# A one-core Strassen weight gradient: another visit order, one pair more, another queue for the last store

## The chip, the cores and the metric

The kernel runs on one core of a Trainium2 chip. TensorE (PE) does the matmuls, VectorE (DVE) and ScalarE (ACT) do the additions and copies, GpSimd (POOL) issues the converting loads, SyncE (SP) issues stores, and 16 DMA engines carry the data. The metric is the device time of one execution in microseconds; lower is better. The kernel before takes 166.42 us, the median of three runs from 166.34 to 166.46. The profile is one execution, whose span from first to last instruction is 164.9 us.

## What is computed

```python
def setup_inputs():
    batch, m, k, n = 16, 512, 1024, 768
    return {
        "input": np.random.randn(batch, m, k).astype(np.float32),
        "grad_output": np.random.randn(batch, m, n).astype(np.float32),
    }

def reference(input, grad_output):
    grad_weight = np.einsum('bmk,bmn->kn', input, grad_output)
    return grad_weight.astype(np.float32)
```

With X of 8192 x 1024 and G of 8192 x 768 this is one matrix product, X transposed times G, of 1024 x 768, contracted over 8192 rows.

## The kernel before, in words

**Output and blocks.** The output is cut into four quadrants of 512 x 384: A (top left), B (top right), C (bottom left), D (bottom right). Each has four pieces q of 128 rows. A piece of 128 x 384 in f32 fits one bank of PSUM; the eight banks make two slots of four, so two quadrants (or two of the Strassen products below) are open at a time. Sums that are not open rest in SBUF: `acc` for A to D, `macc` for the five products m, n, o, p, q.

**Items.** The contraction is cut into 32 units of 256 rows. The string `LOADS` says for each unit how it is used. A unit marked `s` gives two single items of 128 rows; each costs one matmul for each of the 16 pieces of the output, so 32 matmuls a unit. A unit marked `P` is a Strassen pair: its two halves of 128 rows and the two halves of X's and G's columns are the 2 x 2 blocks of one Strassen step, with seven products instead of eight. Each product has four pieces, so 28 matmuls a unit. Two of the products are added straight to A and D; the other five are gathered in m, n, o, p, q. For a pair, DVE first makes six operand sums: `sum_g1` to `sum_g3` of G's blocks and `sum_x1` to `sum_x3` of X's (lines 124 to 153). Products need some of them: m needs g2 and x2, n and q need x1, o and p need g3, A and D need x3 and g1.

**Loads.** GpSimd issues all loads but the first ones, and the DMA turns f32 into bf16. Units below `MERGED` are loaded in two halves of 128 rows (lines 110 and 112), later ones whole (lines 105 and 106). 14 units fit the ring of buffers. The first two tiles of X and the first of G come as f32 through SyncE's and ScalarE's queues and are rounded by DVE and ScalarE (`round_by`, line 202).

**The order.** All engines run in an order written out by hand in `ORDER`. A step such as `3D29!3,0,0,0` is one visit: take 3 operand sums from the list `filler` first, then multiply into D all of its items up to the 29th, then close (the `!`), that is, empty the four banks into SBUF; the four numbers say how many sums DVE takes in ahead of each piece's emptying. A number after a colon (`A28:2`) gives the last pieces of the visit to ScalarE: if the sum was there before, ScalarE copies it from SBUF into the bank ahead of the matmuls (the opening, line 267), and copies the bank back afterwards (line 291). The other pieces are added by DVE from the bank to SBUF (line 295), or copied by it the first time (line 293). A visit without `!` leaves the quadrant open for the next one.

**The end.** After the last pair the five products are shared out to the quadrants: `SHARES` lists 24 additions of `macc` to `acc`, on DVE. Each quadrant's last emptying is followed by its store, issued by SyncE (line 299). In the very last piece the columns are cut into 256 and 128, with one addition and one store each (lines 327, 335 and 336). Ten matmuls of 512 columns and two of 128 run at the start on a constant, to warm up TensorE's clock (line 88).

Of the kernel before, what the change touches and what calls it, by code (L numbers as in the profile page):

```python
# [1 line left out]

# [5 lines left out]

P = 128

LOADS = "ssssssssPPPPPPPPPPPPPPPPPPPPPsss"

ORDER = (
# [10 lines left out]
).split()  # L26


SHARES = (
    "t10 t11 t12 t13 l20 t20 t21 t22 t23 l21 l22 l23 l10 l11 l12 l13 l30 l31 l32 l33 t30 t31 t32 "  # L30
    "t33 "
).split()

WARMUP = [512] * 10 + [128] * 2
PAIRS_HELD = 14
SUMS_HELD = 9

MERGED = 7


@with_exitstack
def kernel(
# [6 lines left out]
    nc = tc.nc  # L49
# [4 lines left out]
    _, _, N = grad_output.shape  # L54
    S = B * M // P
    KH = K // 2
    NH = N // 2
    Q = KH // P
# [3 lines left out]
    OUT = out.rearrange("(ks p) n -> p ks n", p=P)  # L62
# [7 lines left out]
    acc = accp.tile([P, 2 * Q, N], f32, name="acc")  # L70

    macc = accp.tile([P, 5, Q, NH], f32, name="macc")
    SLOT = {"n": 0, "p": 1, "m": 2, "o": 3, "q": 4}
# [23 lines left out]
    items = []  # L97
# [56 lines left out]

    def settled(row, q):
        for p, (_, banks) in opened.items():
            assert p not in ("CD" if row else "AB") or not banks[q][1]

    def share(row, slots, q):
        settled(row, q)  # L160
        dst = acc[:, row + q, :].rearrange("p (h n) -> p h n", h=2)
        nc.vector.tensor_add(out=dst, in0=dst, in1=macc[:, slots, q, :])  # L162

    def top1(q):
        share(0, slice(2, 4), q)

    def top2(q):
        share(0, slice(1, 5, 3), q)

    def top3(q):  # L170
        settled(0, q)
        c = acc[:, q, 0:NH]
        nc.vector.tensor_sub(out=c, in0=c, in1=macc[:, 4, q, :])  # L173

    def low1(q):
        share(Q, slice(0, 3, 2), q)

    def low2(q):
        share(Q, slice(1, 4, 2), q)

    def low3(q):
        settled(Q, q)
        c = acc[:, Q + q, NH:N]
        nc.vector.tensor_sub(out=c, in0=c, in1=macc[:, 0, q, :])

    filler = []
    for i, item in enumerate(items):
        if item[0] == "P":
            filler += [(f, i) for f in (sum_g1, sum_g2, sum_g3, sum_x1, sum_x2, sum_x3)]
    share_by = {"t1": top1, "t2": top2, "t3": top3, "l1": low1, "l2": low2, "l3": low3}  # L190
    filler += [(share_by[c[:2]], int(c[2:])) for c in SHARES]
    filler.reverse()

    def fill(n):
# [20 lines left out]
    streams = {  # L215
        p: [i for i, item in enumerate(items) if item[0] in KINDS.get(p, "P")] for p in "ABCDmnopq"
    }

    LAST_PAIR = max([i for i, item in enumerate(items) if item[0] == "P"], default=0)

    def operands(p, i, q):
        kind, x, g = items[i]
# [16 lines left out]
    def sum_of(p, q):  # L239
        if p in SLOT:  # L240
            return macc[:, SLOT[p], q, :]
        row = q if p in "AB" else Q + q
        return acc[:, row, 0:NH] if p in "AC" else acc[:, row, NH:N]
# [3 lines left out]
    slots = [0, 1]  # L247
    used = set()

    def visit(p, upto, byact, close, ahead, last):  # L250
        items_now = streams[p][done[p] : upto]
        done[p] = upto
        opening = p not in opened
        if opening:

            tail = p in "ABCD" and streams[p][upto - len(items_now)] > LAST_PAIR - 2
            slot = slots.pop(0)
            banks = []
            for q in range(Q):
                name = f"bank{slot * Q + q}"  # L260
                bank = psum.tile([P, 512], f32, name=name)[:, 0:NH]
                act = q >= Q - byact
                carried = act and not fresh[p]
                assert not (carried and tail)
                if carried:
                    assert name in used
                    nc.scalar.copy(out=bank, in_=sum_of(p, q))  # L267
                used.add(name)
                banks.append((bank, carried, act))
            opened[p] = (slot, banks)  # L270
        slot, banks = opened[p]
        final = upto == len(streams[p])

        def mm(q, j):
            stat, mov = operands(p, items_now[j], q)
            bank, carried, _ = banks[q]
            nc.tensor.matmul(  # L277
                bank,
                stat,
                mov,  # L280
                start=opening and j == 0 and not carried,
                stop=close and j == len(items_now) - 1,
                skip_group_check=carried,
            )

        def shut(q):
            fill(ahead[q])
            bank, _, act = banks[q]
            dst = sum_of(p, q)
            if act:  # L290
                nc.scalar.copy(out=dst, in_=bank)  # L291
            elif fresh[p]:
                nc.vector.tensor_copy(out=dst, in_=bank)  # L293
            else:
                nc.vector.tensor_add(out=dst, in0=bank, in1=dst)  # L295
            if final and p in "ABCD":
                row = q if p in "AB" else Q + q
                c0 = 0 if p in "AC" else NH
                nc.sync.dma_start(out=OUT[:, row, c0 : c0 + NH], in_=dst)

        if len(items_now) == 1:
            for q in range(Q):
                mm(q, 0)
            if close:
                for q in range(Q):
                    shut(q)
        else:
            for q in range(Q):
                if last and q == Q - 1 and opening:
                    break  # L310
                for j in range(len(items_now)):
                    mm(q, j)
                if close:
                    shut(q)
            else:
                q = None
            if q is not None:

                fill(ahead[q])
                dst = sum_of(p, q)  # L320
                row = q if p in "AB" else Q + q
                b0 = 0 if p in "AC" else NH
                for c0, c1, name in ((0, 256, None), (256, NH, f"bank{slots[0] * Q}")):
                    bank = banks[q][0] if name is None else psum.tile([P, 512], f32, name=name)
                    for j in range(len(items_now)):
                        stat, mov = operands(p, items_now[j], q)
                        nc.tensor.matmul(
                            bank[:, 0 : c1 - c0],
                            stat,
                            mov[:, c0:c1],  # L330
                            start=j == 0,
                            stop=j == len(items_now) - 1,
                        )
                    d = dst[:, c0:c1]
                    nc.vector.tensor_add(out=d, in0=bank[:, 0 : c1 - c0], in1=d)  # L335
                    nc.sync.dma_start(out=OUT[:, row, b0 + c0 : b0 + c1], in_=d)
        if close:
            fresh[p] = False
            del opened[p]
            slots.append(slot)  # L340

    for n, step in enumerate(ORDER):
        step, _, ahead = step.partition("!")
        step, _, byact = step.partition(":")
        at = next(c for c in step if c.isalpha())
        before, upto = step.split(at)
        if n == 1:
            round_by("DVE", g0, gf, NH, N)
        if n == 2:
            round_by("DVE", x1, xf[1], 4 * P, 6 * P)  # L350
            round_by("ACT", x1, xf[1], 6 * P, 8 * P)
            round_by("DVE", x1, xf[1], 0, 2 * P)
            round_by("ACT", x1, xf[1], 2 * P, 4 * P)
        fill(int(before or 0))
        ahead = [int(a) for a in ahead.split(",")] if ahead else None
        visit(at, int(upto), int(byact or 0), ahead is not None, ahead, n == len(ORDER) - 1)
    assert not filler and not opened


# [28 lines left out]
```

## Time and profile before

| | before |
|---|---|
| time, median of 3 | 166.42 us |
| span of the profile | 164.9 us |
| TensorE busy, instructions | 158.8 us, 958 (12 of them warm-up) |
| DVE busy, instructions | 114.3 us, 231 |
| ScalarE busy, instructions | 83.1 us, 196 |
| mean granted TensorE clock | 0.996 |
| loads | 58.72 MB read |

The busy time of an engine is the sum of the durations of its instructions, and matmuls overlap: one of 384 columns lasts 0.327 us, while the next starts half of that later. So what counts is the distance between the starts of matmuls, and the holes between them. The chain of waits follows the work that ended last back to the start: where it leaves TensorE, TensorE was waiting. The rows of DMA issues give the time from the issue of a transfer to its landing.

### The profile page before, as it was taken

The numbers are of one execution on the slowest core, as the hardware profiler recorded it, in microseconds if no ns is written. First come the engines' busy times: TensorE is split into PE (matmuls) and PEld (weight loads), VectorE is DVE, ScalarE is ACT, GpSimd is POOL, SyncE is SP. The second block draws the span as 40 slices with busy tenths as digits, with TensorE's granted clock in tenths as the row PEclk, the third lists the DMA queues.
The fourth block names the chain that finished last, engine by engine and source line by source line (L and its number), as shares of the span: only waits on it lengthen the run. The fifth ranks groups of instructions, "written<-read, shape, count | busy, mean of one in ns | idle before, by whom it ended". The sixth has DMA issues, their size and how long they took to land.

```text
span 164.9 us, 2645 instructions
## 1 busy us (share of the span) xinstructions
PE 158.8 (96%) x958; PEld 93.8 (57%) x958; DVE 114.3 (69%) x231; ACT 83.1 (50%) x196; POOL 39.9 (24%) x79
## 2 busy tenths in 40 slices
PE   8999999999999999999999999999999999999991
PEld 2456556566545656555566566545656566566560
DVE  0602222002969678879997997998858979999992
ACT  3554442150726586875766744357645568970000
POOL 7444535432222222222222222222122000000000
PEclk9999999999999999999999999999999999999998
DMA  5999999999999999999999999999999999300875
GB/s 179 294 207 208 209 207 210 208 218 209 220 209 216 213 209 218 211 208 221 208 212 213 213 213 214 213 210 215 213 216 212 215 211 214 75 0 0 288 284 191
DMA packets 13836, 33.39 MB, mean 203 GB/s; under 512 B 1536, under 2 KB 5632, under 8 KB 13824
## 3 DMA queue, kind: packets, MB, share of 16 engines
q0 software_dynamic: 10800, 28.64, 89.0%
q1 hardware_dynamic: 2736, 3.54, 6.2%
q10 hardware_dynamic: 288, 1.05, 1.6%
q8 instruction: 7, 0.11, 0.3%
q14 instruction: 5, 0.04, 0.1%
HBM read 58.72 MB, written 3.15 MB: 375 GB/s over the span
## 4 chain that ended last, share of the span: by engine, by line
PE 91%; DVE 6%; issue 1%; DVEq 0%
PE bank L277 88%; PE bank L88 3%; DVE acc L295 3%; DVE xe L144 1%; DVE acc L293 1%; DVE macc L295 1%; DVE acc L173 0%; DVE xp L153 0%; DVE acc L335 0%; DVE xe L148 0%; DVEq L383 0%
## 5 line engine op out<-in xcount | busy, mean ns | idle before, releaser
L277 PEld LDWEIGHTS <-xp 128*128 128x128 bf16 x682 | 66.7, 98 | 46.1 <-issue 1.3
L277 PE MATMUL bank<-gp,xp 128*128 128x384 bf16 x514 | 88.4, 328 | 0.3 <-DVE acc L293 0.2
L291 ACT COPY macc<-bank 128x384 f32<-128x384 f32 x63 | 27.5, 488 | 26.8 <-PE bank L277 26.6
L295 DVE TENSOR_TENSOR acc<-bank,acc 128x384 f32<-128x384 f32 x39 | 19.9, 553 | 28.0 <-PE bank L277 27.7
L291 ACT COPY acc<-bank 128x384 f32<-128x384 f32 x48 | 21.3, 485 | 35.7 <-PE bank L277 35.2
L277 PEld LDWEIGHTS <-xe 128*128 128x128 bf16 x252 | 24.4, 98 | 17.4 <-DVE xe L144 1.5
L277 PE MATMUL bank<-ge,xp 128*128 128x384 bf16 x168 | 31.1, 327 | 0.7 <-DVE xp L153 0.7
L277 PE MATMUL bank<-gp,xe 128*128 128x384 bf16 x168 | 30.4, 327 | 0.6 <-DVE xe L144 0.6
L106 POOL DMA_DIRECT2D xp<-in_input_dram x25 | 13.2, 527 | 41.8 <-DMA xp<-in_input_dram 24.3
L105 POOL DMA_DIRECT2D gp<-in_grad_output_dram x25 | 13.2, 527 | 31.8 <-DMA gp<-in_grad_output_dram 11.4
L295 DVE TENSOR_TENSOR macc<-bank,macc 128x384 f32<-128x384 f32 x29 | 15.2, 554 | 6.6 <-PE bank L277 6.3
L267 ACT COPY bank<-macc 128x384 f32<-128x384 f32 x43 | 19.2, 505 | 0.0
L267 ACT COPY bank<-acc 128x384 f32<-128x384 f32 x36 | 16.1, 497 | 0.0
L144 DVE TENSOR_TENSOR xe<-xp 128x1024 bf16<-128x1024 bf16 x21 | 14.4, 685 | 1.9 <-DMA xp<-in_input_dram 1.9
L277 PE MATMUL bank<-ge,xe 128*128 128x384 bf16 x84 | 15.5, 327 | 0.0
L153 DVE TENSOR_TENSOR xp<-xp 128x1024 bf16<-128x1024 bf16 x21 | 14.4, 685 | 0.0
L162 DVE TENSOR_TENSOR acc<-acc,macc 128x768 f32<-128x768 f32 x16 | 14.1, 953 | 0.0
L130 DVE TENSOR_TENSOR ge<-gp 128x768 bf16<-128x768 bf16 x21 | 11.6, 552 | 0.8 <-DMA gp<-in_grad_output_dram 0.8
L139 DVE TENSOR_TENSOR gp<-gp 128x768 bf16<-128x768 bf16 x21 | 11.6, 552 | 0.0
L148 DVE TENSOR_TENSOR xe<-xp 128x512 bf16<-128x512 bf16 x21 | 8.8, 419 | 0.0
L112 POOL DMA_DIRECT2D xp<-in_input_dram x12 | 6.5, 538 | 9.0 <-DMA xp<-in_input_dram 6.8
L110 POOL DMA_DIRECT2D gp<-in_grad_output_dram x13 | 7.1, 549 | 3.8 <-DMA gp<-in_grad_output_dram 3.1
(18 smaller groups left out, 27.6 us busy)
## 6 DMA issues: line engine op xcount, KB each, us to landing
xp<-in_input_dram POOLq DMA_DIRECT2D x25, 512.0 KB, 16.9
gp<-in_grad_output_dram POOLq DMA_DIRECT2D x25, 384.0 KB, 16.7
xp<-in_input_dram POOLq DMA_DIRECT2D x12, 256.0 KB, 8.5
out_dram<-acc SPq DMA_DIRECT2D x15, 192.0 KB, 2.1
gp<-in_grad_output_dram POOLq DMA_DIRECT2D x13, 192.0 KB, 8.5
xf<-in_input_dram ACTq DMA_DIRECT2D x2, 512.0 KB, 4.9
gf<-in_grad_output_dram SPq DMA_DIRECT2D x2, 192.0 KB, 4.4
out_dram<-acc SPq DMA_DIRECT2D x1, 128.0 KB, 1.9
```

What stands on the lines that cost most here:

```text
L105: nc.gpsimd.dma_start(out=gp, in_=G[rows, :].rearrange("(p m) n -> p m n", m=2))
L106: nc.gpsimd.dma_start(out=xp, in_=X[rows, :].rearrange("(p m) k -> p m k", m=2))
L130: nc.vector.tensor_add(out=ge[:, 0:2, :], in0=g[:, :, 0, :], in1=g[:, :, 1, :])
L139: nc.vector.tensor_sub(out=g[:, 1:3, :], in0=g[:, 1:3, :], in1=g[:, 3::-3, :])
L144: nc.vector.tensor_add(out=xe[:, 0:2, :].rearrange("p a k -> p (a k)"), in0=xp[:, 0, :], in1=xp[:, 1, :])
L148: nc.vector.tensor_add(out=extra[i][0][:, 2, :], in0=xp[:, 0, 0:KH], in1=xp[:, 1, KH:K])
L153: nc.vector.tensor_sub(out=x[:, 1:3, :], in0=x[:, 1:3, :], in1=x[:, 0::3, :])
L162: nc.vector.tensor_add(out=dst, in0=dst, in1=macc[:, slots, q, :])
L267: nc.scalar.copy(out=bank, in_=sum_of(p, q))
L277: nc.tensor.matmul(bank, stat, mov, start=opening and j == 0 and not carried, stop=close and j == len(items_now) - 1, skip_group_check=car ...
L291: nc.scalar.copy(out=dst, in_=bank)
L295: nc.vector.tensor_add(out=dst, in0=bank, in1=dst)
```

## The change

One unit more is a Strassen pair, so 22 pairs and 20 singles instead of 21 and 22. The visit order and the order of the shares are new; they were found by a search over orders that uses durations measured on the chip and takes the stores into account. `MERGED` is 2 instead of 7. A visit can now open its banks with one of the five products itself: `C20:0+n` copies n from `macc` into the banks of C on ScalarE, and the shares of n to C are then left out (`taken`). The rounding of the second tile stands ahead of the first visit that needs it. The store of the last 128 columns is issued by ScalarE. The aim is fewer matmuls and fewer waits of TensorE. The core of the diff:

```diff
-LOADS = "ssssssssPPPPPPPPPPPPPPPPPPPPPsss"
+LOADS = "ssssssssPPPPPPPPPPPPPPPPPPPPPPss"
 
 
 
 ORDER = (
-    "A1:4 C1:2!0,0,0,0 D1:2 A2!0,0,0,0 D2 B3:4 D3 D4!0,0,0,0 B4 C4:2 C5 B5 C6!0,0,0,0 B6 A6:2 B7 "
-    "A8!0,0,0,0 D8:2 B8 B9 D10!0,0,0,0 B10 B11 C7:2 C9 B12 C11 B13!0,0,0,0 C12 C13 A14:2 C14 "
-    "C16!0,0,0,0 A15 B16:2!3,0,0,0 D16:2 3A17!3,0,0,1 n2:4!0,1,1,0 D17 D18 m2:4!3,0,1,0 "
-    "q3:4!1,1,1,1 D19 o1:4 o2 o3 1o4!2,1,0,0 D20!0,0,0,0 p4:4 n3:3 3p5!3,0,0,0 n4 A21:2!3,0,0,1 "
-    "n6 1m6:4!3,1,0,1 n7 o7:2!2,0,0,1 q7:2!2,0,0,2 n8 p8:2!2,0,0,1 D24:2!1,1,0,2 n9 A25:3!3,0,1,1 "
-    "n10 o10:2!2,0,0,1 m10:2 2n11!2,0,0,1 m11 q11:2!2,0,1,1 p12:2!1,1,0,2 D28:2 m12 3D29!3,0,0,0 "
-    "m13 A28:2 2m14!1,0,0,0 A30 o12:2 o13 3o15!3,0,0,1 A31 q15:2!2,1,0,2 A32!0,0,0,0 n16:2 "
-    "D32:4!6,1,1,1 p17:2 1n18!3,0,0,0 p18 m17:2 2p19!3,0,0,0 m19 D35:3!3,1,0,2 o20:2 m20 "
-    "3o21!2,0,0,0 m21!0,0,0,0 q20:2 p20:4 p21!4,1,0,0 q21!0,0,0,0 D39:0 n21:4!3,1,0,1 D41 "
-    "A37:4!2,1,1,1 D42 B17:0 D43!6,0,0,0 B19 B22!0,0,0,0 C19:0 C22!0,0,0,0 A43:0!4,0,0,0 "
+    "C1:4!0,0,0,0 D1:1 A2:2!0,0,0,0 D2!0,0,0,0 B2:2 C3:1 B4!0,0,0,0 C4!0,0,0,0 A3 A4!0,0,0,0 D4 "
+    "D5 A6:4!0,0,0,0 D6!0,0,0,0 B6:1!0,0,0,0 C7!0,0,0,0 A8:1 D8:1 D10!0,0,0,0 A10!0,0,0,0 B10:2 "
+    "B12!0,0,0,0 C12 D13:3!0,0,0,0 A13:1!0,0,0,0 C16!0,0,0,1 1B16:4!0,0,0,0 D14 2A16:3!1,0,3,0 "
+    "D17 3m2:4!2,0,0,1 D18!0,0,0,0 n2:4!1,0,1,0 1q2:4!0,3,0,0 2o3:2 p2:3 o4!0,0,0,1 p4 1A19:4 "
+    "3A20!0,0,3,0 p5 q5!0,0,0,0 m5:4!1,0,2,0 p6!1,1,0,1 n6!0,0,0,1 o6:4 D22:4 9D23 4o8!1,0,0,0 "
+    "A24:2!0,0,0,0 2q8:1 q9!1,0,0,0 D25!0,2,0,0 p7 1p8 p10!1,0,2,0 m7:4 m10!0,0,6,0 o11!0,1,0,0 "
+    "3n10:4 p12:3!3,1,0,0 n12!1,0,2,0 q12:1 m13:4!6,0,0,0 q13!0,0,0,0 1A28 1A29!0,1,0,2 D30:4 "
+    "o14:4 o15!0,1,1,0 D31!0,2,4,0 2p16 1A32:3!0,0,0,0 3n17!0,2,0,1 p17!0,0,0,0 2D33:3 q16:4 "
+    "1q18!0,0,1,1 2m16 2D35!0,0,7,0 m19 2m20!0,0,0,0 o20:4 5p19:2 1p21 o21 o22!0,2,0,0 "
+    "1p22!0,0,0,3 A36 m22:4!0,0,0,1 A38 q20:3 q22!3,0,0,0 1A40 n20:4 1n22!0,0,0,3 3A42!0,0,1,0 "
+    "C20:0+n!0,0,0,1 B20:4!3,1,1,1 D42!0,0,1,0 "
 ).split()
 
 
 SHARES = (
-    "t10 t11 t12 t13 l20 t20 t21 t22 t23 l21 l22 l23 l10 l11 l12 l13 l30 l31 l32 l33 t30 t31 t32 "
-    "t33 "
+    "l20 l21 l22 l23 t10 t11 t12 t13 t20 t21 t22 t30 t31 t32 t23 t33 l30 l10 l11 l12 l31 l32 l13 "
+    "l33 "
 ).split()
 
 WARMUP = [512] * 10 + [128] * 2
 PAIRS_HELD = 14
 SUMS_HELD = 9
 
-MERGED = 7
+MERGED = 2
...
-    def visit(p, upto, byact, close, ahead, last):
+    def visit(p, upto, byact, first, close, ahead, last):
         items_now = streams[p][done[p] : upto]
         done[p] = upto
         opening = p not in opened
         if opening:
-
-            tail = p in "ABCD" and streams[p][upto - len(items_now)] > LAST_PAIR - 2
             slot = slots.pop(0)
             banks = []
             for q in range(Q):
@@ -261,12 +262,20 @@
                 bank = psum.tile([P, 512], f32, name=name)[:, 0:NH]
                 act = q >= Q - byact
                 carried = act and not fresh[p]
-                assert not (carried and tail)
                 if carried:
                     assert name in used
                     nc.scalar.copy(out=bank, in_=sum_of(p, q))
+                elif first:
+                    assert name in used and not fresh[p] and not byact
+                    src = macc[:, SLOT[first[1]], q, :]
+                    if first[0] == "-":
+                        nc.scalar.mul(out=bank, in_=src, mul=-1.0)
+                    else:
+                        nc.scalar.copy(out=bank, in_=src)
                 used.add(name)
-                banks.append((bank, carried, act))
+                banks.append((bank, carried or bool(first), act))
+            if first:
+                taken.add((p, first[1]))
             opened[p] = (slot, banks)
...
-                    nc.sync.dma_start(out=OUT[:, row, b0 + c0 : b0 + c1], in_=d)
+                    store = nc.sync if name is None else nc.scalar
+                    store.dma_start(out=OUT[:, row, b0 + c0 : b0 + c1], in_=d)
...
-        if n == 2:
+        if not rounded and done[at] < 2 <= int(upto):
+            rounded = True
```

More of the change, by code (lines that the diff above doesn't have):

```diff
@@ L1 @@
 from contextlib import ExitStack
+from functools import partial
 import concourse.bass as bass
@@ L156, in settled, with share @@
         for p, (_, banks) in opened.items():
-            assert p not in ("CD" if row else "AB") or not banks[q][1]
-    def share(row, slots, q):
-        settled(row, q)
[L161 to L184, printed above, removed]
+            assert p not in ("CD" if row else "AB") or not (banks[q][1] and banks[q][2])
+    SHARE_OF = {
+        "t1": ("m", "o", 0),
+        "t2": ("p", "q", 0),
+        "t3": ("q", None, 0),
+        "l1": ("n", "m", Q),
+        "l2": ("p", "o", Q),
+        "l3": (None, "n", Q),
+    }
+    taken = set()
+    def share(name, q):
+        left, right, row = SHARE_OF[name]
+        sides = [
+            (h, p)
+            for h, p in enumerate((left, right))
+            if p and ("ABCD"[(row > 0) * 2 + h], p) not in taken
+        ]
+        settled(row, q)
+        if len(sides) == 2:
+            a, b = SLOT[left], SLOT[right]
+            dst = acc[:, row + q, :].rearrange("p (h n) -> p h n", h=2)
+            src = macc[:, a : b + 1 : b - a, q, :]
+        else:
+            ((h, p),) = sides
+            dst = acc[:, row + q, h * NH : (h + 1) * NH]
+            src = macc[:, SLOT[p], q, :]
+        op = nc.vector.tensor_sub if name[1] == "3" else nc.vector.tensor_add
+        op(out=dst, in0=dst, in1=src)
     filler = []
@@ L189 @@
             filler += [(f, i) for f in (sum_g1, sum_g2, sum_g3, sum_x1, sum_x2, sum_x3)]
-    share_by = {"t1": top1, "t2": top2, "t3": top3, "l1": low1, "l2": low2, "l3": low3}
-    filler += [(share_by[c[:2]], int(c[2:])) for c in SHARES]
+    filler += [(partial(share, c[:2]), int(c[2:])) for c in SHARES]
     filler.reverse()
@@ L217 @@
     }
-    LAST_PAIR = max([i for i, item in enumerate(items) if item[0] == "P"], default=0)
     def operands(p, i, q):
@@ L267, in visit @@
                     nc.scalar.copy(out=bank, in_=sum_of(p, q))
+                elif first:
[3 more added lines that the diff above has]
+                        nc.scalar.mul(out=bank, in_=src, mul=-1.0)
+                    else:
+                        nc.scalar.copy(out=bank, in_=src)
                 used.add(name)
-                banks.append((bank, carried, act))
+                banks.append((bank, carried or bool(first), act))
+            if first:
+                taken.add((p, first[1]))
             opened[p] = (slot, banks)
@@ L309, in visit @@
                 if last and q == Q - 1 and opening:
+                    assert not banks[q][1]
                     break
@@ L340, in visit @@
             slots.append(slot)
+    rounded = False
     for n, step in enumerate(ORDER):
@@ L344 @@
         step, _, byact = step.partition(":")
+        byact, first = byact[:1], byact[1:]
         at = next(c for c in step if c.isalpha())
@@ L355 @@
         ahead = [int(a) for a in ahead.split(",")] if ahead else None
-        visit(at, int(upto), int(byact or 0), ahead is not None, ahead, n == len(ORDER) - 1)
+        visit(at, int(upto), int(byact or 0), first, ahead is not None, ahead, n == len(ORDER) - 1)
     assert not filler and not opened
```

## The prediction

> **What bounds the kernel now.** I read the busy table and the slices first, then the chain of waits piece by piece, then the DMA issues of single loads, then the last two microseconds in order of time.
>
> ```profile
> span 164.9 us, 2645 instructions
> PE 158.8 (96%) x958; PEld 93.8 (57%) x958; DVE 114.3 (69%) x231; ACT 83.1 (50%) x196; POOL 39.9 (24%) x79
> DMA  5999999999999999999999999999999999300875
> ```
>
> TensorE is busy from the second slice to the last but one, and so is the DMA until slice 35. DVE has room on average only. The chain shows where TensorE lost time.
>
> ```profile
> 5.42 1.45 PE bank L277 x5
> 6.89 1.03 DVE acc L293 x2
> 7.97 39.99 PE bank L277 x245
> 47.98 1.02 DVE acc L295 x2
> 49.00 0.61 DVE xe L144
> 49.65 59.30 PE bank L277 x363
> 108.98 0.56 DVE macc L295
> 109.54 0.60 DVE xe L144
> 110.14 0.47 DVE macc L295
> 110.61 0.33 DVE xe L148
> 110.94 0.61 DVE xp L153
> 111.60 44.23 PE bank L277 x271
> 155.84 2.02 DVE acc L295 x4
> ```
>
> In the last PE piece 270 steps take 44.23 us less the 0.33 of the last matmul: 0.1626 us for 384 columns. Where the chain leaves PE, PE waited. The matmul starts in order of time have four places far above 0.1625: two holes at 7.01 and 7.50 (0.33 and 0.30 too much: the second visit to a bank pair waits for the evictions of C1), 48.75 (0.74: n2 waits for the sum of L144), 75.34 (0.12, the same for n8) and 110.57 (0.87: A32 waits for L153 of the last pair it takes, behind two evictions and two other sums on DVE). So 1.73 us is lost after the head, all to sums that DVE makes too late. At the end DVE carries the chain, and then the store queue:
>
> ```profile
> 160.69 0.50 PE L327 MATMUL bank<-gp,xp 128*128 128x128 bf16 x6
> 161.05 0.61 DVE L335 TENSOR_TENSOR acc<-bank,acc 128x256 f32<-128x256 f32 x2
> 161.62 0.90 SPq L336 DMA_DIRECT2D out_dram<-acc  x2
> out_dram<-acc SPq DMA_DIRECT2D x1, 128.0 KB, 1.9
> out_dram<-acc SPq DMA_DIRECT2D x1, 64.0 KB, 1.7
> ```
>
> The last matmul starts at 160.69 + 5 x 0.055 = 160.97; call this L. The last addition ends at 161.66, but its store is issued at 162.12, since SyncE is issuing the store before it until 162.03. It lands at 163.77, L + 2.80; the exit takes 1.10 more.
>
> **What the skill says.** "TensorE: Matmul & The Clock Gate", Back-to-back issue gap: N/2.4 + 2.5 ns when warm, 162.5, 109.2 and 55.8 ns at 384, 256 and 128 columns; the trace has 162.6, 109 and 55. The same page (What's actually happening) wants some 3.4 us of idling before the clock drops again, so a hole of 0.2 us behind the warm-up should not cost the clock; before shows no such hole. "DMA: Bandwidth & Descriptors", Issuing engines are not separate DMA queues: a second issuing engine saves only issuing time. Before can't show that for stores; the SyncE wait above is such time.
>
> **Part 1, matmuls.** A pair costs 7 x 4 = 28 matmuls where two single tiles cost 32. 21 pairs and 22 singles are 588 + 352 = 940 pieces, 22 and 20 are 616 + 320 = 936. The last column block is cut in two over 7 items instead of 6, so full pieces go from 934 to 929 and cut ones from 6 + 6 to 7 + 7: -5 x 0.1625 + 0.109 + 0.055 = **-0.65 us**.
>
> **Part 2, the head.** C1 comes first and needs the third DVE cast of x0 (over at 5.38) instead of the first (5.12): first matmul at 5.43, not 5.21. Three cold steps of 0.32 and one of about 0.38 on the way to warm bring D1 to 6.77, where it also waits for the cast of the right half of g0 (over at 6.73). D1 runs to 7.45. A2 uses the banks of C1, which ScalarE begins to empty at about 6.0; they follow each other 0.37 apart, and the last is free at 7.63, before its turn. x1 lands at 6.97 and DVE, free now, casts it by 7.5 (before: from 7.83, behind two evictions). Matmul number 16 comes at 8.75; before, number n comes at 6.50 + 0.1625 n, so 9.10. **-0.35 us**: both head holes are gone, and the line becomes 6.15 + 0.1625 n.
>
> **Part 3, the loads.** MERGED falls from 7 to 2: units 2 to 6 land whole, where their first halves came 2.2 us earlier. When TensorE arrives on the line above, and when the second half of the same unit landed before:
> - unit 2 (D5, number 64): 16.55, against 7.71 + 8.5 = 16.25
> - unit 3 (C7, number 90): 20.78, against 12.12 + 8.5 = 20.65
> - unit 4 (D10, number 116): 25.00, against 16.53 + 9.2 = 25.77
>
> ```profile
> xp<-in_input_dram POOLq DMA_DIRECT2D x1, 256.0 KB, 8.5
> xp<-in_input_dram POOLq DMA_DIRECT2D x1, 256.0 KB, 9.2
> ```
>
> (The issues at 7.71 and at 16.53.) The 0.7 extra on the last is one of the 16 engines: a 16 KB fetch of instructions at 21.54 takes it for 0.95 us and all later landings wait for that engine. The changed program has as many TensorE instructions, so I keep it. In before a unit takes 4.42 us unmerged and 4.33 merged, so three merged units come about 0.3 earlier: wait at D10 0.77 - 0.3, **+0.5 us** (0 to 0.9). It also swallows whatever is lost before it. Later units have room: unit 29 is asked for at number 784, 6.15 + 127.4 + 0.5 = 134.05 or later, against 134.16 before and some 0.4 less now.
>
> **Part 4, sums, openings, evictions.** I wrote the order of DVE and ScalarE beside TensorE's numbers, each instruction at the later of its turn and its inputs plus 0.04, with steps from back-to-back rows: sums 0.47, 0.27, 0.47, 0.60, 0.335, 0.60 (2.74 a pair), evictions 0.465 on DVE and 0.37 on ScalarE, openings (bank from acc or macc) 0.41, shares 0.87 or 0.47. The running sums give for before 0.72, 0.09 and 0.84 at the three late sums, where the trace has 0.74, 0.12 and 0.87. DVE goes from 109 to 126 us in 264 instructions instead of 224 (6 sums, 34 evictions more), ScalarE from 111 to 121 evictions and from 79 to 99 openings: from 43 us on DVE is taken for about 0.9 of the time. Yet the three late sums vanish: pair 17 is summed right after its landing (47.59 by before's times: x1 48.26, x2 48.86, over at 49.28 for m2 at 49.36), D31 is fed before A32, and A32 comes with x3 done. **-1.73 us**. What remains are a dozen places within 0.1 of waiting (D8, A16, m2, A19, p6, A24, p12, q12, q16, m20, n20, C20); the sums give 0.1 us in all with a handover of 0.04 and 0.33 with 0.06. A stationary operand from DVE took 0.09 from the end of the cast to the matmul at 5.2. I take **+0.3 us** (0.1 to 1.0). Opening C from the sum n by ScalarE is a copy at the price of the other openings, and halves four shares; it waits for the last eviction of n22, and behind it stand the openings of B20, asked for 2.6 us later. The new assertions act while the program is built and cost nothing.
>
> **Part 5, the tail.** The six shares of B20 leave DVE free by the second piece of D42, so the last addition starts 0.27 after L instead of 0.42, ends at L + 0.55, and ScalarE, whose work ended 3 us earlier, issues at L + 0.6, with nothing queued behind. With 1.65 it lands at L + 2.25. The 128 KB store stays on SyncE: addition over at L + 0.28, issue L + 0.33, landing L + 2.27. Against L + 2.80: **-0.5 us**.
>
> **Sum.** -0.65 - 0.35 + 0.5 - 1.73 + 0.3 = -1.93 for L (159.0), -0.5 behind it: 166.42 - 2.43 = **164.0 us**.
>
> **Rivals.** (a) Loads hold it more: for, units 2 to 4 have no slack and merging makes TensorE wait for whole units; against, the DMA stream is full in both kernels. A wait of 1.5 instead of 0.5 gives 165.0. (b) DVE at 0.9 turns a dozen touching handovers into a chain: for, each late eviction delays a sum; against, the sums above. At 0.2 each, 2.4 instead of 0.3 gives 166.1; with one more hole of the old size (0.87), 167.0, slower than before. (c) No wait at D10 at all: 163.5; L can't fall far then, because unit 29 becomes the limit (134.16 + 24.7 = 158.9, or 158.5 with loads 0.4 earlier).
>
> **Chances.** Forecast 0.68; (a) 0.11; (c) 0.12; (b) 0.09, of which 0.04 ends slower. Range 163.4 to 165.0: it takes in (c) and (a), the wait of 0 to 0.9 and the handovers of 0.1 to 1.0. Faster 0.94, same 0.02, slower 0.04.
>
> **What would show it.** Right: no hole over 0.15 us on TensorE after 30 us, one before D10 near 25.0 that a load of x ends, matmul 16 at about 8.75, the last store issued by ScalarE 0.06 after the last addition and no later landing by SyncE. Wrong: holes ended by DVE sums or by ScalarE openings that sum to over 1 us, cold matmuls beyond 6.6, or landings of units 2 to 4 later than in before.

## The result, and the profile after

The changed kernel takes 164.69 us, median of four runs (164.59 to 164.82), against 166.44 before (four runs, 166.34 to 166.53): a ratio of 0.9895, 95% interval 0.9878 to 0.9912, so 1.75 us or about one per cent less. The forecast was 164.0 with a range of 163.4 to 165.0.

The page of the changed kernel, its busy times and the row of DMA slices:

```profile
span 163.0 us, 2759 instructions
PE 158.0 (97%) x955; PEld 93.2 (57%) x955; DVE 130.7 (80%) x271; ACT 96.3 (59%) x226; POOL 34.6 (21%) x69
DMA  5999999999999999999999999999999999600894
```

TensorE has three matmuls less, DVE has 16 us more work in a shorter span. That DVE went from 69% to 80% says nothing of the time yet; the chain of waits does (start, length, what):

```profile
2.41 7.21 DMA xp<-in_input_dram
9.62 0.28 issue
9.90 15.93 DMA xp<-in_input_dram
25.84 0.05 issue
25.88 132.81 PE bank L286 x813
158.69 0.78 PE bank L337 x7
159.49 0.68 DVE acc L345 x2
```

Before, the chain left TensorE at 48 and 109 for DVE's sums, and ended on 6 us of DVE. Now, followed back from the end, it leaves TensorE once, at 25.88, and what lies ahead of that is a load: X of unit 4, issued at 9.90, landing at 25.84. From there on TensorE carries the chain to the last 0.7 us. TensorE and the DMA around that place, in order of time (start, length, what; in brackets the idle time before and what ended it):

```profile
23.68 1.46 PE L286 MATMUL bank<-gp,xp 128*128 128x384 bf16 x8
25.88 0.82 PE L286 MATMUL bank<-gp,xp 128*128 128x384 bf16 x4 [0.74 <-DMA xp<-in_input_dram]
```

The bracket has 0.74 because a matmul lasts twice its step; from start to start there is 0.91 too much. The end of the kernel:

```profile
159.49 0.68 DVE L345 TENSOR_TENSOR acc<-bank,acc 128x256 f32<-128x256 f32 x2 [0.21 <-PE bank L337]
159.94 0.33 SPq L347 DMA_DIRECT2D out_dram<-acc  x1
160.21 0.35 ACTq L347 DMA_DIRECT2D out_dram<-acc  x1
```

DVE waits for TensorE here (0.21), where before it was behind. The last matmul starts at 159.63, the last addition ends at 160.17, ScalarE issues at 160.21, and the last landing is at 161.89.

The starts of all matmuls in order, and the last landing, split the 1.88 us by which the span is shorter (0.03 is left over):

| part | forecast | measured |
|---|---|---|
| fewer matmuls | -0.65 | -0.65 (943 for 946, step 0.1625 as before) |
| head: matmul number 16 | 9.10 to 8.75 | 9.10 to 8.73 |
| wait before D10 | +0.5 | +0.91 |
| three late sums | -1.73 | -1.73 (all three gone) |
| small handovers after 30 us | +0.3 | +0.53 (nine holes of 0.02 to 0.13) |
| last matmul to last landing | 2.80 to 2.27 | 2.80 to 2.26 |

The profiled execution of before took 166.66 us, 0.24 more than the median from which the forecast subtracts its terms; that of the changed kernel took 164.76, 0.07 more than its median. So the two profiles differ by 1.90 us and the medians by 1.75.

### The profile page after: what moved, and what is told of

Read it like the earlier page. It is cut to its first block, busy times and chain, and to the rows that moved or that the text cites. A ratio compares the mean times of both kernels' runs of the same rounds, so it can differ in the third digit from the quotient of the medians.

```text
span 163.0 us, 2759 instructions
## 1 busy us (share of the span) xinstructions
PE 158.0 (97%) x955; PEld 93.2 (57%) x955; DVE 130.7 (80%) x271; ACT 96.3 (59%) x226; POOL 34.6 (21%) x69
## 4 chain that ended last, share of the span: by engine, by line
PE 82%; DMA 14%; POOL 1%; issue 1%; DVE 0%; POOLq 0%
PE bank L286 81%; DMA xp<-in_input_dram 14%; POOL gp L112 1%; PE bank L337 0%; DVE acc L345 0%; POOLq L386 0%
## 5 line engine op out<-in xcount | busy, mean ns | idle before, releaser
L286 PE MATMUL bank<-gp,xp 128*128 128x384 bf16 x492 | 84.0, 326 | 1.1 <-DMA xp<-in_input_dram 0.7
L304 DVE TENSOR_TENSOR acc<-bank,acc 128x384 f32<-128x384 f32 x58 | 29.2, 549 | 16.5 <-PE bank L286 15.9
L108 POOL DMA_DIRECT2D xp<-in_input_dram x30 | 15.9, 530 | 52.3 <-DMA xp<-in_input_dram 28.5
L267 ACT COPY bank<-macc 128x384 f32<-128x384 f32 x50 | 22.6, 510 | 6.2 <-DVE macc L304 4.2
L267 ACT COPY bank<-acc 128x384 f32<-128x384 f32 x45 | 20.4, 501 | 6.7 <-DVE acc L304 3.4
L107 POOL DMA_DIRECT2D gp<-in_grad_output_dram x30 | 15.9, 531 | 38.2 <-DMA gp<-in_grad_output_dram 17.2
L304 DVE TENSOR_TENSOR macc<-bank,macc 128x384 f32<-128x384 f32 x38 | 19.1, 549 | 2.9 <-PE bank L286 1.8
L190 DVE TENSOR_TENSOR acc<-acc,macc 128x768 f32<-128x768 f32 (+1 forms) x24 | 16.5, 748 | 0.0
L136 DVE TENSOR_TENSOR ge<-gp 128x384 bf16<-128x384 bf16 x22 | 7.7, 348 | 0.0
L302 DVE COPY acc<-bank 128x384 f32<-128x384 f32 x7 | 3.5, 550 | 2.5 <-PE bank L286 2.4
```

Source lines behind the costliest of these rows:

```text
L107: nc.gpsimd.dma_start(out=gp, in_=G[rows, :].rearrange("(p m) n -> p m n", m=2))
L108: nc.gpsimd.dma_start(out=xp, in_=X[rows, :].rearrange("(p m) k -> p m k", m=2))
L190: op(out=dst, in0=dst, in1=src)
L286: nc.tensor.matmul(bank, stat, mov, start=opening and j == 0 and not carried, stop=close and j == len(items_now) - 1, skip_group_check=car ...
```

## The experiments

The theory: the changed kernel is held by one load (unit 4 at D10), then by small handovers; it gained by the place of the sums on DVE and by the tail. Rivals: the merged loads make that wait; DVE is full, so every hole that is closed opens elsewhere; ScalarE's queue makes the tail. The 0.65 us for the 22nd pair is counted from the matmuls and their step; no run takes that pair back alone.

**C8 for C7.** Four matmuls on a tile that has landed go ahead of D10.

```diff
-B6:1!0,0,0,0 C7!0,0,0,0 A8:1 D8:1 D10!0,0,0,0
+B6:1!0,0,0,0 C8!0,0,0,0 A8:1 D8:1 D10!0,0,0,0
```

> The changed kernel, with C7 made C8: four matmuls of C on item 7, which has landed, stand ahead of A8, D8 and D10 instead of in C12. If the 0.91 us wait at D10 is one for the landing of unit 4 (25.84), TensorE comes to it 4 x 0.1625 = 0.65 later, waits 0.26, and all that follows is 0.65 earlier: 164.05. Rival, the gain is taken back by later waits for DVE sums, whose places have under 0.1 us of room: 164.4 to 164.7.

Measured: 164.25 us (163.97 to 164.47), ratio to before 0.9857 (0.9842 to 0.9872), where the changed kernel has 0.9895: 0.4 less by the medians, 0.6 by the ratios. The forecast was 0.65 less and the rival 0 to 0.3 less, so most of the 0.65 was gained. TensorE at D10 in the profiled execution:

```profile
23.81 2.93 PE L286 MATMUL bank<-gp,xp 128*128 128x384 bf16 x17
```

There are 17 matmuls in a row, and no hole. In that execution the first loads landed 0.33 later and matmul 16 came at 9.35 instead of 8.73, so TensorE came to D10 at 26.25, behind the landing at 25.79. With the head of the changed kernel's profile it would have come at 25.63, some 0.2 ahead of that landing. The kernel with five changed steps, below, has C8 too: there TensorE comes to D10 at 25.76, behind a landing at 25.49, and there is no hole either. The holes after 30 us are the same, to 0.003 us, as in the changed kernel: nothing was taken back. So the wait at D10 is real. As long as it stands, TensorE leaves D10 at the landing, however early its head was.

**The last store on SyncE again.**

```diff
-store = nc.sync if name is None else nc.scalar
+store = nc.sync
```

> The changed kernel, with the last store issued by SyncE again. If only the issue time counts, SyncE is free of the 128 KB store at 160.32 where ScalarE issued at 160.21: 0.1 longer, 164.8. Rival, as the forecast had it for before (SyncE 0.46 late): 0.45 longer, 165.15.

```profile
159.24 0.68 DVE L345 TENSOR_TENSOR acc<-bank,acc 128x256 f32<-128x256 f32 x2 [0.21 <-PE bank L337]
159.70 0.83 SPq L347 DMA_DIRECT2D out_dram<-acc  x2
```

Measured: 164.77 us, ratio 0.9897 (0.9883 to 0.9910): the same time as with ScalarE's queue, within the interval. In the trace the last store is issued 0.74 after the last matmul's start instead of 0.58, and lands at 2.35 instead of 2.26. So in the traces ScalarE's queue is worth 0.1 us, too little for the times to show, since SyncE is no longer behind: its store before the two starts at 159.06 and is over in 0.33.

**MERGED = 7 in the changed kernel.**

```diff
-MERGED = 2
+MERGED = 7
```

> The changed kernel with MERGED = 7, units 2 to 6 in halves again. If merging costs nothing because D10, C7 and D5 need both items of their unit at once or nearly so, 164.7 within 0.15, the wait before D10 about as long. Rival, the whole-unit landing makes the wait: the wait falls by up to 0.9, 163.8 to 164.2.

```profile
26.20 0.99 PE L286 MATMUL bank<-gp,xp 128*128 128x384 bf16 x5 [0.43 <-DMA xp<-in_input_dram]
```

Measured: 164.83 us, ratio 0.9895 (0.9882 to 0.9909), equal to the changed kernel. The hole is there (0.60 from start to start), one matmul later: D10's first matmul needs item 8 and its second item 9, whose half of the unit landed at 26.16 in that execution. The hole is shorter than 0.91 because matmul 16 came 0.47 later there. Merging whole units is not what makes TensorE wait.

**The kernel before with two visits' sums ahead of its evictions.**

```diff
-3A17!3,0,0,1
+3A17!4,0,0,0
-q15:2!2,1,0,2
+q15:2!5,0,0,0
```

> The kernel before, with two visits changed: 3A17!3,0,0,1 becomes 3A17!4,0,0,0 and q15:2!2,1,0,2 becomes q15:2!5,0,0,0, so the same sums stand ahead of the DVE evictions of the visit instead of between and behind them. If the order on DVE made the holes at n2 (0.74) and A32 (0.87), A32's goes wholly and n2's falls to about 0.2, with some 0.15 turning up at n7: 1.2 less than before, 165.2. Rival, DVE has too much to do there and a later place pays: 166.2 or more.

Measured: 165.74 us, ratio 0.9953 (0.9940 to 0.9965): 0.8 less than before, not 1.2. A32's hole (0.87) is gone: at 110.6 TensorE runs on. At n2 the order gained less than expected:

```profile
32.95 14.91 DMA xp<-in_input_dram
47.86 0.02 issue
47.88 0.69 DVE xe L144
48.58 0.48 DVE acc L295
49.05 0.04 issue
49.09 1.93 PE bank L277 x10
```

The sum of pair 17 now goes first, but its tile lands at 47.86 (47.59 in the profile of before), and the eviction of A17, whose bank n2 opens, stands behind it. The holes are 0.64 and 0.14 instead of 0.74, but TensorE came to n2 at 48.46 here and at 48.91 in before, because matmul 16 came at 8.42 instead of 9.10. What counts is when n2 goes on: its third matmul starts at 49.56 instead of 49.82, so 0.26 was gained there where 0.5 was expected. At n7 0.17 turned up. So order alone closed the hole at A32, where DVE's inputs were there; at n2, where the sum waits for a load, it closed only a part. No second hole paid for A32.

**Five steps of the C8 kernel changed, so that sums or evictions come a little earlier.**

```diff
-2o3:2
+2o3:1
-A24:2!0,0,0,0
+A24:1!0,0,0,0
-p10!1,0,2,0
+3p10!0,0,0,0
-3n17!0,2,0,1
+5n17!1,0,0,0
-2D35!0,0,7,0
+2D35!3,0,1,3
```

> The C8 kernel of the first group with five more steps changed, which move operand sums ahead of evictions or give one piece more to DVE: o3:1, A24:1, 3p10!0,0,0,0, 5n17!1,0,0,0, 2D35!3,0,1,3. The changed kernel has ten holes of 0.02 to 0.13 after 30 us, 0.54 in sum. If each is a handover between DVE or ScalarE and TensorE that comes a little late, those at A19, A24, q12, q16 and m20 (0.32 in sum) go, those at p6, A16 and C20 stay: 0.3 less than with C8 alone, 163.95. Rival, DVE is full and the holes move to other visits: the same as C8 alone, 164.25.

Measured: 163.84 us, ratio 0.9833 (0.9820 to 0.9847), the fastest of all and 0.4 less than C8 alone. The holes after 30 us are A16 0.03, p6 0.13, one of 0.06 ahead of q12's fourth piece (0.02 before) and C20 0.05; those at A19, A24, q12's first piece, q16 and m20 are gone. Their sum is 0.27 instead of 0.53, so 0.26 of the 0.4 is theirs; the intervals of the two ratios overlap, and the rest is not explained. The chain:

```profile
7.71 149.93 PE bank L286 x920
157.65 0.78 PE bank L337 x7
158.45 0.68 DVE acc L345 x2
```

From 7.71 to the last additions the chain stays on TensorE; holes as small as these don't break it. DVE is busy for 132.1 us of the span of 161.9, more than in any other kernel here, and yet only 0.04 of the holes moved on, to q12's fourth piece: the rival of the full DVE falls.

**More short warm-ups.** What delays unit 4? A load's landing is told in 16 steps, one for each DMA engine as I read it. In the changed kernel 15 of the 16 engines have landed it by 24.77, before TensorE comes to it at 24.98; the last is at 25.84. A transfer of the instruction kind, 16 KB, is on one engine from 21.27 for 0.95 us.

```diff
-WARMUP = [512] * 10 + [128] * 2
+WARMUP = [128] * 42
```

> The changed kernel with 42 warm-up matmuls of 128 columns instead of ten of 512 and two of 128: the same 4.5 us of warm-up, but 30 matmuls and weight loads more ahead of everything. If the late landing of unit 4 comes from TensorE's own fetch of instructions (16 KB over one of the 16 engines, at 21.3 in the changed kernel), the fetch comes 30 x 0.1625 = 4.9 earlier, at about 16.4, the last of the 16 engines lags from then on, unit 3 lands at 21.2 or later instead of 20.5 and a hole of about 0.6 appears at C7, and the hole at D10 is shorter by that; the time stays near 164.7. Rival, the lag belongs to the loads or to the clock time: it begins at 21 to 23 as before, and C7 has no hole.

Measured: 165.40 us, ratio 0.9926 (0.9911 to 0.9941): 0.5 to 0.7 more than the changed kernel, where no change was expected. The fetch is at 15.83, and the hole moved with it, further than expected, to D5:

```profile
14.72 2.28 PE L286 MATMUL bank<-gp,xp 128*128 128x384 bf16 x13
17.91 0.82 PE L286 MATMUL bank<-gp,xp 128*128 128x384 bf16 x4 [0.92 <-DMA xp<-in_input_dram]
```

Unit 2 is complete on 15 engines by 16.29 and on the last at 17.87; TensorE loses 1.08 there, and nothing at C7 or D10, where it is now late itself. In the changed kernel the last engine is 0.01 behind at the landing of 20.49 and 1.18 at the next, 23.48, with the fetch at 21.27 between them; here it is 0.04 behind at 13.83 and 1.58 at 17.87, with the fetch between them too. So the lag follows the place in TensorE's program, not the loads. My time for it was wrong. In the profiled execution, 0.96 slower than that of the changed kernel, the last matmul starts at 160.11 instead of 159.63: 0.30 of this is the head (matmul 16 at 9.03), 0.18 the larger hole. The last store also took 2.16 from issue to landing instead of 1.68; why, I don't know, and so it stays open what makes the medians differ.

**The kernel before with the tail of the change alone.** ScalarE opens and empties C's last visit, and issues the last store.

```diff
-C19:0
+C19:4
-                assert not (carried and tail)
-nc.sync.dma_start(out=OUT[:, row, b0 + c0 : b0 + c1], in_=d)
+store = nc.sync if name is None else nc.scalar
+store.dma_start(out=OUT[:, row, b0 + c0 : b0 + c1], in_=d)
```

> The kernel before with C19:4 instead of C19:0 (ScalarE opens and empties the four banks of C's last visit, so DVE has four evictions less in the last 10 us) and the last store issued by ScalarE; nothing else. If the tail of 2.80 us from the last matmul to the last landing is DVE's queue and SyncE's queue, it becomes 2.3 as in the changed kernel: 0.45 to 0.5 less than before, 166.0. Rival, the tail is the transfer itself: the same time as before.

```profile
160.96 0.63 DVE L334 TENSOR_TENSOR acc<-bank,acc 128x256 f32<-128x256 f32 x2
161.41 0.33 SPq L336 DMA_DIRECT2D out_dram<-acc  x1
161.62 0.35 ACTq L336 DMA_DIRECT2D out_dram<-acc  x1
```

Measured: 166.18 us, ratio 0.9971 (0.9959 to 0.9984), 0.47 less. The last matmul starts at 161.04 as before, the last landing is at 163.36: 2.32 after it, as forecast. With the 0.1 of the store's queue taken off, as the other kernel showed it, 0.35 to 0.4 is left for DVE: its own queue, and stores that come in time for SyncE to be free. That share is a difference of two runs, not a run of its own.

## Why the prediction was right, and where its sizes were off

The direction, the mechanism and the range were right; the gain was 1.75 where 2.43 was forecast. Two terms hold the difference between the profiles, which is 1.90. The other 0.15 is the base of the sum: the median, 0.24 below the profile from which the terms were read.

- **Part 3, the loads, "wait at D10 0.77 - 0.3".** The 0.3 for merging did come in this profile: 15 engines landed unit 4 at 24.77, where in before the second last was at 25.07 (25.07 again in that of C8, whose first loads were 0.33 late). But the lag of the one engine, which I kept at 0.7, was 1.07 in the profiled execution (0.69 to 0.78 in those of C8, of the store on SyncE and of the five steps). The landing was at 25.84, the wait 0.91: I had 0.41 too little. Unit 4 landed 0.07 later than in before, so one of the forecast's own signs of being wrong came up, if barely. With the store on SyncE the wait was 0.54, so the forecast of 0.5 lies within what executions do; a single profile gave too narrow a view of it.
- **Part 4, "I take +0.3".** It was 0.53. Of the dozen places named, eight show holes (A16, A19, p6, A24, q12, q16, m20, C20), and q12 has a second one ahead of its fourth piece. In the profiles that keep this order they are the same to 0.003 us, but for that second one, which is not there with `MERGED` at 7. p6 alone is 0.13. DVE's lines ahead of it:

```profile
63.12 2.02 DVE L304 TENSOR_TENSOR macc<-bank,macc 128x384 f32<-128x384 f32 x4 [0.93 <-ACT acc L300]
65.05 0.55 DVE L132 TENSOR_TENSOR ge<-gp 128x768 bf16<-128x768 bf16 x1
65.52 0.35 DVE L136 TENSOR_TENSOR ge<-gp 128x384 bf16<-128x384 bf16 x1
65.79 0.55 DVE L141 TENSOR_TENSOR gp<-gp 128x768 bf16<-128x768 bf16 x1
```

  The four evictions of q5 follow TensorE's pieces, and the three sums follow them without a gap; p6 starts at 66.39, 0.05 after the last. But each of the evictions waits for TensorE and for ScalarE, and the trace has a wait instruction of its own ahead of it: the last at 64.51, and the eviction starts at 64.58. These 0.07 were in no handover of mine, and 0.05 + 0.07 is nearly the 0.13. This is read from the trace; no run takes the second wait away, and for the other places the cause stays open.
- **Parts 1 and 2** came out to 0.02 us, part 1 by its count, part 2 in part by luck. In the head errors cancel: the clock was full at 5.5, earlier than before's 6.55, and in the place of cold steps stood two waits, 0.46 at D1 for the cast of the right half of g0 (over at 6.52, not 6.73) and 0.20 at matmul 9 for DVE's cast of x1 (over at 7.52). And matmul 16 came at 8.73 to 9.35 in the five profiles of the changed head with the old warm-up, at 8.42 to 9.18 in the three of the old head, so one pair of profiles can't show 0.35.
- **The clock and the step.** The idling of 0.2 us after the warm-up came before the clock was full, so it tests nothing. A better case is the run with `MERGED` at 7: the clock is recorded full from 3.86 on and stays so, though TensorE idles for some 0.9 us before its first matmul at 5.50 and for 1.07 ahead of D1. At the end the clock falls 2.6 to 4.5 us after the start of the last matmul, in the seven profiles that record it. The Trainium skill ("TensorE: Matmul & The Clock Gate", What's actually happening) has the clock fall after some 3.4 us of idling: the first agrees with it, the second lies on both sides of it. On the step, the same page (Back-to-back issue gap) gives the formula of the prediction for isolated matmuls alone, and 131 ns at 512 columns for a stream with weight loads; the stream here has 162.5 ns at 384 columns, as the formula has it, and the measurement decides.
- **The three late sums** went as forecast. The run on before shows at A32 that the place in DVE's order made the hole, not the amount of DVE's work; at n2 it shows so in part.
- **Part 5, the tail**, was right in size and in both its reasons, but I gave no shares: 0.1 is ScalarE's queue, the rest DVE's. The Trainium skill, "DMA: Bandwidth & Descriptors", Issuing engines are not separate DMA queues, which says that a second issuer saves only issuing time, fits: the store on SyncE was issued 0.16 later and landed 0.09 later.
- **The rivals**: (b), that DVE's handovers become a chain, did not happen with DVE at 80% nor at 82%; (a) was nearest, with a wait between the forecast's and its own. The signs named for being right came: the largest hole after 30 us is 0.13, the one before D10 ends with a load of x, and ScalarE issues the last store 0.04 after the last addition.

## What to carry to other kernels

When DVE feeds TensorE, its busy share says little: an operand sum behind two evictions cost 0.87 us with DVE at 69%, and with DVE at 82% all holes after 30 us together cost 0.27. Give each load the room of its slowest engine, and put work on tiles that have landed ahead of the first matmul on a new one: four matmuls moved were worth 0.4 to 0.6 us. A second queue for the last store was worth 0.1 us once the stores before it came in time; look first at the engine that feeds the store.

## What the runs showed of the hardware that I had not expected

TensorE's program comes over the same 16 DMA engines as the data. Each 16 KB of it is one transfer, which took 0.88 to 0.98 us in the profiles of the two kernels, 16 to 25 us apart. Loads that are striped over all 16 then wait for one engine: at X of unit 4, in the changed kernel and the runs made from it with the old warm-up, it came 0.69 to 1.07 us after the other 15, and 1.58 us at X of unit 2 in the run with short warm-ups, the first load to land after the fetch there. Why the lag can be longer than the fetch stays open. Thirty matmuls more at the start moved the fetch from 21.27 to 15.83 and the wait from D10 to D5. The time at which TensorE's clock became full differed from 3.5 to 6.6 us between six executions with the same warm-up. DVE's evictions of q5 wait for two engines, and each has a wait instruction of its own, which starts 0.07 us ahead of it.
